# One set of weight sums fewer, a longer wait for the early sums in the output projection, and half a weight unit moved behind the turned tiles

## The chip, the core and the metric

The kernel runs on one core of one Trainium2 chip. The metric is the device time of one execution in microseconds; lower is better. Before the change the median of three runs is 1202.67 us (1201.94 to 1203.7). The profile shown below is of one further execution, which took 1203.26 us; its span, from the first to the last instruction that the profile shows, is 1201.4 us. So 1.86 us lie around the span.

Engine names: PE is the matmul engine (PEld its weight loads), DVE the vector engine, ACT the scalar engine, POOL is used mostly for its DMA queue, and SP only issues DMAs.

## What is computed

One decoder layer over 256 tokens of width 2048, all in float32. The part that matters here, cut from the reference:

```python
h += concat(A, B) @ W_o               # A: latent attention, B: block attention
h += SwiGLU(RMSNorm(h))               # W_gate, W_up: 2048 x 5632, W_down: 5632 x 2048
h += sigmoid(RMSNorm(h) @ W_pg) * (p[i] @ W_pe)
final RMSNorm
```

## The kernel before

Every weight is read once from memory, in **units** of 256 weight rows by 1024 columns (1 MB), and multiplied with the 256 tokens, which stay on the chip. A float32 product is made of three matmuls of reduced precision (`three`, lines 400 to 402): the high part of the activation times the high part of the weight, low times high, high times low. So each weight tile must first be split into two parts: ACT writes the high part (`split_hi`, line 352, a cast), DVE the low part (`split_lo`, line 363, a subtraction). The parts go into a ring of slots (`ringh`/`ringl`, then `moreh`/`morel`, then the two halves of `most`), and a slot is free again when PE has read it. The third matmul of a product (line 402) is the one that reads the low part.

Stages follow each other in program order: the attention's projections and attention itself, the output projection in two column halves `wo0` and `wo1` (eight units each), the norm and transposes for the feed-forward part, then gate and up groups in column blocks of 1024: `g0`, `u0`, `g1`, one half of down (`d10`), `u1`, the other half (`d11`), `g2` and so on.

Some units of a gate or up group are multiplied by **Strassen's scheme**: seven products of half size instead of eight (`seven`). Such a unit, written S, needs sums of its weight quarters, and is split in four jobs: "11 22" (two quarters, 1024 columns), "21" (512), and the sums "t1 t3" and "t4 t2" (1024 each). PE takes them in four turns: two products (6 matmuls), one (3), two (6), two (6), so 21 matmuls for a unit. The sums are made in one of two ways:
- **in line**: DVE makes them in place, in the raw tile, between its splits of the same unit: line 362 (1024 columns), then lines 365 and 366 (512 each);
- **early**: the generator `early_sums` (lines 370 to 388) loads the weights over POOL's queue during attention and output projection (line 378), waits until PE has been given a set number of columns (`wait()`), lets DVE make the sums (lines 384 to 386, `wsums`) and stores them to memory (line 388). Later the unit is loaded as three quarters (lines 224 and 225) and its sums (line 226), into two raw tiles. `EARLY` (line 1044) says how many S units of each group are early: 14 before.

`S["two"]` chooses the wait of `early_sums`: 57344 columns in the groups ga, q0 and u0 (the latent's up-projection of the attention part also has the names u0 and u1), else 34816. PE starts a matmul of 512 columns every 0.227 us in the trace.

Each engine's list of instructions is written out by hand, in program order: the last loop of the program walks over the units; for each it collects the jobs that may be split now (`todo`, at most two or three units ahead), issues their splits, then the unit's products, and then the loads of raw tiles that have come free. Of the last unit of the first up group `u0`, the splits are woven between its products (`WOVEN`). That unit ends the group: its evacuation adds the Strassen part (line 430, `U`), multiplies with the gate (line 1012, `stage`), and PE turns the result (`ff_transpose`, line 1032) into banks, from which ACT and DVE write the **turned tiles** `ffTh` (line 121) and `ffTl` (line 122). The next group `g1` has the units "6 S0 S1 S2 S3 S4 S5 7", of which S4 and S5 are early. The matmuls of unit S0 write banks that `ffTl` must have read first.

In the output projection, the products of `wo0` are added to `h` by DVE (line 899, four instructions, one for each bank), and the first products of `wo1` write the same four banks again. Behind it come the statistics of the first norm (lines 169 to 180), ACT's scaling (line 952) and PE's transposes (line 138).

Of the kernel before, what the change touches and what calls it, by code (L numbers as in the profile page):

```python
# [35 lines left out]
def kernel(ctx, tc, x, p, positions, attn_norm, w_in, kv_norm, w_ukv, w_o, ffn_norm,  # L36
# [31 lines left out]
    def load_x(dst, c0, c1):  # L68
        nc.sync.dma_start(dst[:, :, c0:c1], x_v[:, :, c0:c1])
# [114 lines left out]
    units = []  # L184
# [28 lines left out]
    def load(i):  # L213
        if i >= len(units) or units[i].again or i in raw:
            return
        u = units[i]
        u.asked = asking[0]
        while max(u.raw, u.raw2) >= len(raws):
            n = len(raws)
            raws.append(big.tile([128, 2048], F32, name=f"raw{n}", tag=f"f1{'hl'[n - 3]}"))  # L220
        if u.early:
            r = raws[u.raw][:, 0:1536]
            (w, c0, _), k0 = u.srcs[0], u.ks[0] * 128
            nc.sync.dma_start(r[:, 0:512], w[k0:k0 + 128, c0:c0 + 512])
            nc.sync.dma_start(r[:, 512:1536], w[k0 + 128:k0 + 256, c0:c0 + 1024])
            nc.sync.dma_start(raws[u.raw2], u.early)
            raw[i] = r.rearrange("q (a c) -> q a c", a=3)
            return
        n = sum(c1 - c0 for _, c0, c1 in u.srcs)
        nk = len(u.ks)  # L230
        r = raws[u.raw][:, 0:nk * n].rearrange("q (k c) -> q k c", k=nk)
        o = 0
        for w, c0, c1 in u.srcs:
            k0 = u.ks[0]
            nc.sync.dma_start(r[:, :, o:o + c1 - c0],
                              w[k0 * 128:(k0 + nk) * 128, c0:c1].rearrange("(k q) c -> q k c", q=128))
            o += c1 - c0
        raw[i] = r
# [6 lines left out]
    jobs, turns = [], []  # L245
# [124 lines left out]
    def early_sums(tag, enough, wait):  # L370

        made = 0
        while todo_early and made < enough:
            u = todo_early.pop(0)
            made += 1
            f = big.tile([128, 4, 512], F32, name="wsums", tag=tag)
            (w, c0, _), k0 = u.srcs[0], u.ks[0] * 128
            nc.gpsimd.dma_start(f.rearrange("q (k a) c -> q k (a c)", k=2),
                                w[k0:k0 + 256, c0:c0 + 1024].rearrange("(k q) c -> q k c", q=128))
            since = columns[0]  # L380
            while columns[0] < since + wait() or S["crowded"]:
                yield 1
            tt = nc.vector.tensor_tensor
            tt(f[:, 0:2], f[:, 1:2].to_broadcast([128, 2, 512]), f[:, 0:4:3], op=ALU.subtract)
            tt(f[:, 3], f[:, 3], f[:, 0], op=ALU.subtract)
            tt(f[:, 2], f[:, 2], f[:, 3], op=ALU.subtract)
            u.early = dram.tile([128, 2048], F32, name=f"wsums{u.name}{u.idx}")
            nc.gpsimd.dma_start(u.early, f.rearrange("q a c -> q (a c)"))

    def split(jb):  # L390
        if not jb.cast:
            split_hi(jb)
        split_lo(jb)
# [85 lines left out]
    def sums_of(parts, k0, pairs, at, tag="vb"):  # L479

        for n, kk in enumerate(pairs):
            both = big.tile([128, 2, 2, SEQ], F32, name="both", tag=tag)
            whole, some = both[:, 0], both[:, 1]
            h, l = (x[:, kk - k0:kk - k0 + 2] for x in parts)
            tt = nc.vector.tensor_tensor
            tt(whole, h.bitcast(F32), l.bitcast(F32), op=ALU.add)
            a11, a21, a12, a22 = (whole[:, i, t * 128:(t + 1) * 128] for i in range(2) for t in range(2))
            hi, lo = (aT[i][:, at + 2 * n:at + 2 * n + 2] for i in range(2))
            four = some.rearrange("q a (b c) -> q (a b) c", b=2)
            tt(four[:, 0], a21, a22, op=ALU.add)  # L490
            tt(four[:, 1], four[:, 0], a11, op=ALU.subtract)
            tt(four[:, 2], a21, a11, op=ALU.subtract)
            tt(four[:, 3], a12, four[:, 1], op=ALU.subtract)
            split_psum(hi, lo, some)
            yield 1
# [10 lines left out]
    def add(gen, wait=0, front=False):  # L506
        tasks.insert(0 if front else len(tasks), [wait, gen])
# [143 lines left out]
    S = {"done": 0, "doneB": 0}  # L651
# [389 lines left out]

    wg, wup, wd = w_gate[0], w_up[0], w_down[0]

    EARLY = dict(u0=2, g1=2, u1=2, g2=1, u2=2, g3=1, u3=2, u4=2)

    def mixed(name, order=((0, 0), (1, 0), (0, 1), (1, 1))):

# [5 lines left out]
                    adding=tuple(i for i, x in enumerate(pairs) if x[-1] == "+"),  # L1053
                    early=sevens[-EARLY.get(name, 0):] if name in EARLY else (), order=list(order) if sevens else None,
                    swap=not sevens, deep=True)
# [34 lines left out]
    def h_back():  # L1090
        S["h"] = big.tile([128, NT, D], F32, name="h", tag="xh")
        nc.gpsimd.dma_start(S["h"], S["hd"])
# [150 lines left out]
    for n in range(3):  # L1243
        for i in range(4):
            if n:
                u = Unit()
# [42 lines left out]
    nxt, j = 2, 0  # L1289
    coming = 3  # L1290

    def loads(end):

        nonlocal coming
        while coming < end and (units[coming].again or units[coming].behind < (
                jobs[nxt].unit if nxt < len(jobs) else len(units))):
            load(coming)
            coming += 1

    for i, u in enumerate(units):  # L1300
        asking[0] = i
        if i < wide:
            load(i + 3)
        S["two"] = u.name in ("ga", "q0", "u0")
        S["crowded"] = u.name == "v" and u.idx > 0 or u.name == "wo0" and u.idx < 4
        if u.name == "ga" and u.idx == 5:
            todo_early.extend(x for x in units if x.early)
            add(early_sums("f0l", 2, lambda: 53248))
        if u.name == "ga" and u.idx == 8:
            add(early_sums("more_sums", 99, lambda: 57344 if S["two"] else 34816))  # L1310
        if u.name == "g1" and u.idx == 0:
            S["mid"] = S.pop("turned")
        if u.name == "wo0":
            S["twice"] = u.idx < 4
        if i < 5:
            load_x(xt, 768 + 256 * i, 1024 + 256 * i)
        if u.name == "dl0" and u.idx == 1:
            h_back()
        if u.name == "dl0" and u.idx == 0:
            add(sums_of(ffT[4], 32, LAST_SUMS, 8), 5)  # L1320
        if u.name == "dl0" and u.idx == 2:
            add(p_load())
        if u.name == "pg0" and u.idx == 0:
            fg_load()
        if u.name == "wo0" and u.idx < 4:
            step()
        for n in range(max(1, len(u.turns))):
            todo, late = [], []
            while i not in raw and u.turns:
                loads(i + 1)  # L1330
            while nxt < len(jobs) and jobs[nxt].unit in raw and jobs[nxt].wait < j and jobs[nxt].unit <= i + (3 if i > 1 else 1) and \
                    (jobs[nxt].unit <= i + 2 or i >= wide and units[jobs[nxt].unit].asked < i) and \
                    not (u.sevens_end and 0 <= n < 3 and jobs[nxt].unit > i + 1) and \
                    not (jobs[nxt].unit > i + 2 and i + 1 < len(units) and units[i + 1].name == "u0" and units[i + 1].mixed and units[i + 1].last):
                todo.append(jobs[nxt])
                nxt += 1
            weave = u.name in WOVEN and u.last
            if "mid" in S and not u.strassen and u.mixed or u.sevens_end and n == 3 or weave:
                late = [jb for jb in todo if jb.turn > j]
                todo = [jb for jb in todo if jb.turn <= j]  # L1340
            if i >= 5:
                high_parts(todo + late if weave else todo)
            if i == 2:
                product(u, [0])
            if n % 2 == 0:
                step()
            for jb in todo:
                if i < 3:
                    for c0, c1 in units[jb.unit].chunks:
                        split_hi(jb, c0, c1, len(jb.kks))  # L1350
                        split_lo(jb, c0, c1, len(jb.kks))
                    continue
                split(jb)
            while posts:
                posts.pop()()
            if u.strassen:
                seven(u, n)
            elif i == 2:
                product(u, [1])
            else:  # L1360
                product(u, [kk for jb in u.turns[n] for kk in jb.kks] if u.turns else range(len(u.ks)), late if weave else ())
            if "mid" in S and not u.strassen and u.mixed and 2 * u.idx + n >= 0 and len([*S["mid"]]) >= 0:
                S.pop("mid")
            high_parts(late)
            for jb in late:
                split(jb)
            loads(len(units) if i >= wide else wide + 3)
            j += not u.again
# [25 lines left out]
```

## Time and profile before

| | |
|---|---|
| median of three runs | 1202.67 us |
| the profiled execution | 1203.26 us |
| its span | 1201.4 us |
| DVE busy | 948.4 us (79%) |
| ACT busy | 712.6 us (59%) |
| POOL busy | 57.3 us (5%) |
| read from memory, written | 254.08 MB, 27.26 MB |

Busy time is the time in which an engine works on some instruction. The views used below are: the page (busy shares, and the clock that was granted to PE in 40 slices of the span), the list of waits by engine, the timeline (start in us, length in us, engine, line, operation, output and inputs, count of merged instructions; in brackets the engine's idle time before and what ended it), the same work grouped by shape in a window, the chain of work that ended last, and busy times by window. A row that merges several instructions gives the time from the start of the first to the end of the last.

### The profile page before, as it was taken

Reading aid. Unit: us, or ns where it says so; the run is one execution under the profiler, and the core shown is the slowest. Engines: PE = TensorE matmul, PEld = TensorE weight load, DVE = VectorE, ACT = ScalarE, POOL = GpSimd, SP = SyncE. Lnnn points to the kernel's source line nnn. Section 1 sums busy time; section 2 is a strip of 40 time slices with the busy share of each in tenths; the row PEclk is TensorE's granted clock in tenths of the full one; section 3 lists DMA queues with packets and bytes.
Section 4 is the critical chain, followed back from the end, with each engine's and each line's share of the span. In section 5 each row is a group of like instructions: output and inputs, shape, how many; then the busy total and the mean of one; then the engine's idle time right before and its main releaser. Section 6 shows DMA issues by size and latency. Waiting matters only on the chain.

```text
span 1201.4 us, 14608 instructions
## 1 busy us (share of the span) xinstructions
PE 1177.2 (98%) x5480; PEld 983.9 (82%) x5480; DVE 948.4 (79%) x1119; ACT 712.6 (59%) x908; POOL 57.3 (5%) x80
## 2 busy tenths in 40 slices
PE   9999999999979999899999999999999999999996
PEld 7888888899868888688888888888888888888886
DVE  5675756776556687998999899989998999897474
ACT  6735745456546656475757675756566665565453
POOL 5310000000000000000000000000000000000000
PEclk9999999999989999899999999999999999999998
DMA  8896877755675677296887788787959795936631
GB/s 300 283 339 215 283 284 255 273 184 212 226 299 194 252 231 291 102 333 197 320 235 261 221 314 238 258 248 272 264 201 266 253 290 189 358 126 228 209 105 71
DMA packets 87799, 290.69 MB, mean 242 GB/s; under 512 B 5740, under 2 KB 10144, under 8 KB 82864
## 3 DMA queue, kind: packets, MB, share of 16 engines
q1 hardware_dynamic: 77984, 240.94, 56.4%
q0 software_dynamic: 9456, 48.29, 14.7%
q8 instruction: 43, 0.70, 0.2%
q10 hardware_dynamic: 288, 0.52, 0.1%
q14 instruction: 28, 0.23, 0.1%
HBM read 254.08 MB, written 27.26 MB: 234 GB/s over the span
## 4 chain that ended last, share of the span: by engine, by line
PE 94%; DVE 3%; DMA 2%; ACT 0%; issue 0%; SPq 0%; DVEq 0%
PE bank L400 30%; PE bank L402 30%; PE bank L401 30%; PE bank L138 1%; DMA wsumsu<-wsums 1%; PE bank L593 1%; DMA wsums<-in_w_up 1%; PE bank L1032 1%; DVE ringl L363 1%; PE bank L714 1%; DMA x<-in_x 1%; PE bank L622 1%; PE bank L616 0%; PE bank L596 0%; PE bank L623 0%
## 5 line engine op out<-in xcount | busy, mean ns | idle before, releaser
L352 ACT CAST ringh<-raw 128x1024 fp32r<-128x1024 f32 (+4 forms) x307 | 372.7, 1249 | 279.2 <-PE bank L401 117.4
L363 DVE TENSOR_TENSOR ringl<-raw,ringh 128x1024 fp32r<-128x1024 f32 (+4 forms) x307 | 443.9, 1468 | 110.9 <-ACT ringh L352 108.7
L400 PE MATMUL bank<-ringh,aT 128*128 128x512 f32 (+3 forms) x713 | 275.0, 386 | 0.0
L402 PE MATMUL bank<-ringl,aT 128*128 128x512 f32 (+3 forms) x713 | 270.5, 379 | 0.2 <-DVE ringl L363 0.2
L401 PE MATMUL bank<-ringh,aT 128*128 128x512 f32 (+3 forms) x713 | 270.0, 379 | 0.0
L402 PEld LDWEIGHTS bank<-ringl,aT 128*128 128x128 f32 x713 | 133.9, 188 | 25.5 <-DVE ringl L363 1.1
L400 PEld LDWEIGHTS bank<-ringh,aT 128*128 128x128 f32 x713 | 134.2, 188 | 23.6 <-ACT aT L124 0.3
L401 PEld LDWEIGHTS bank<-ringh,aT 128*128 128x128 f32 x713 | 134.1, 188 | 23.4
L352 ACT CAST moreh<-raw 128x1024 fp32r<-128x1024 f32 (+2 forms) x70 | 79.8, 1174 | 22.5 <-DVE raw L362 9.2
L363 DVE TENSOR_TENSOR morel<-raw,moreh 128x1024 fp32r<-128x1024 f32 (+2 forms) x66 | 85.5, 1317 | 0.6
L352 ACT CAST most<-raw 128x1024 fp32r<-128x1024 f32 (+2 forms) x58 | 56.7, 1006 | 42.1 <-DVE raw L362 16.0
L400 PE MATMUL bank<-ringh,ffTh 128*128 128x512 f32 x204 | 79.4, 389 | 0.0
L401 PE MATMUL bank<-ringh,ffTl 128*128 128x512 f32 x204 | 79.4, 389 | 0.0
L402 PE MATMUL bank<-ringl,ffTh 128*128 128x512 f32 x204 | 79.4, 389 | 0.0
L363 DVE TENSOR_TENSOR most<-raw,most 128x1024 fp32r<-128x1024 f32 (+2 forms) x58 | 66.3, 1164 | 2.4 <-ACT most L352 2.3
L362 DVE TENSOR_TENSOR raw<-raw 128x1024 f32<-128x1024 f32 x50 | 61.2, 1225 | 1.7
L402 PEld LDWEIGHTS bank<-ringl,ffTh 128*128 128x128 f32 x204 | 38.3, 188 | 7.9
L401 PEld LDWEIGHTS bank<-ringh,ffTl 128*128 128x128 f32 x204 | 38.3, 188 | 7.9
L400 PEld LDWEIGHTS bank<-ringh,ffTh 128*128 128x128 f32 x204 | 38.3, 188 | 7.9
L400 PE MATMUL bank<-most,aT 128*128 128x512 f32 x88 | 35.2, 400 | 5.9 <-DVE ffTl L122 5.9
L366 DVE TENSOR_TENSOR raw<-raw 128x512 f32<-128x512 f32 x50 | 34.6, 692 | 1.7
L402 PE MATMUL bank<-most,aT 128*128 128x512 f32 x88 | 34.7, 395 | 0.0
(353 smaller groups left out, 1970.7 us busy)
## 6 DMA issues: line engine op xcount, KB each, us to landing
raw<-in_w_down SPq DMA_DIRECT2D x44, 1024.0 KB, 7.4
raw<-in_w_gate SPq DMA_DIRECT2D x36, 1024.0 KB, 7.7
raw<-in_w_up SPq DMA_DIRECT2D x30, 1024.0 KB, 8.7
raw<-in_w_in SPq DMA_DIRECT2D x40, 512.0 KB, 4.7
raw<-in_w_o SPq DMA_DIRECT2D x16, 1024.0 KB, 5.4
raw<-in_w_ple_gate SPq DMA_DIRECT2D x16, 1024.0 KB, 5.0
wsums<-in_w_up POOLq DMA_DIRECT2D x10, 1024.0 KB, 6.1
wsumsu<-wsums POOLq DMA_DIRECT2D x10, 1024.0 KB, 4.8
```

Of the source, the lines that this page charges most:

```text
L138: nc.tensor.transpose(b[:, (2 * i + t) * 128:(2 * i + t + 1) * 128], part[:, t, i * 128:(i + 1) * 128], ident)
L352: nc.scalar.copy(h[:, :, c0:c1], r[:, :, c0:c1])
L362: tt(f[:, 0:2], f[:, 1:2].to_broadcast([128, 2, 512]), f[:, 0:4:3], op=ALU.subtract)
L363: tt(l[:, :, c0:c1], r[:, :, c0:c1], h[:, :, c0:c1].bitcast(F32), op=ALU.subtract)
L366: tt(f[:, 2], f[:, 2], f[:, 3], op=ALU.subtract)
L400: nc.tensor.matmul(b, xh, h, start=start, stop=False)
L401: nc.tensor.matmul(b, xl, h, start=False, stop=False)
L402: nc.tensor.matmul(b, xh, l, start=False, stop=stop)
L593: nc.tensor.matmul(s[:, c0:c0 + nk], qT[:, q * 128:(q + 1) * 128], kT[:, 0:nk], start=True, stop=qpe is None)
L622: nc.tensor.matmul(o[:, 0:256], v(0), pT[:, 0:256], start=True, stop=False)
L714: nc.tensor.transpose(b[:, (2 * i + t) * 128:(2 * i + t + 1) * 128], src[:, t, col(i0 + i):col(i0 + i) + 128], ident)
L1032: nc.tensor.transpose(b[:, (2 * i + t) * 128:(2 * i + t + 1) * 128], st[:, t, (k + i) * 128:(k + i + 1) * 128], ident)
```

## The change

Three edits. `EARLY` takes one S unit of `u0` instead of two (S3; S2 now makes its sums in line), so there are 13 early sets. The long wait of 57344 columns now holds in `wo0` and `wo1` too, where it was 34816. And the rule for which jobs wait beyond `u0`'s end is a function: as before, at the last unit but one of `u0` no job further than two units ahead is taken; new is that at its last unit none of S1 of `g1` is taken, and of S0 only the first two jobs.

```diff
-    EARLY = dict(u0=2, g1=2, u1=2, g2=1, u2=2, g3=1, u3=2, u4=2)
+    EARLY = dict(u0=1, g1=2, u1=2, g2=1, u2=2, g3=1, u3=2, u4=2)
...
+    end_u0 = next(i for i, u in enumerate(units) if u.name == "g1") - 1
+
+    def may_wait(i, jb):
+        return i == end_u0 - 1 and jb.unit > i + 2 or i == end_u0 and (
+            jb.unit > i + 2 or jb.unit == i + 2 and jb.kind in ("t1 t3", "t4 t2"))
...
-        S["two"] = u.name in ("ga", "q0", "u0")
+        S["long"] = u.name in ("ga", "q0", "u0", "wo0", "wo1")
...
-            add(early_sums("more_sums", 99, lambda: 57344 if S["two"] else 34816))
+            add(early_sums("more_sums", 99, lambda: 57344 if S["long"] else 34816))
...
-                    not (jobs[nxt].unit > i + 2 and i + 1 < len(units) and units[i + 1].name == "u0" and units[i + 1].mixed and units[i + 1].last):
+                    not may_wait(i, jobs[nxt]):
```

PE's order of instructions is the same before and after. What moves on DVE, first at the end of `wo0` (raw_112 to raw_114 are the three raw tiles of that stage, bank_77 to bank_80 the banks of `wo0`):

```order
 L363 TENSOR_TENSOR ringl<-raw_113,ringh 128x2048
-L384 TENSOR_TENSOR wsums<-wsums 128x1024
-L385 TENSOR_TENSOR wsums<-wsums 128x512
-L386 TENSOR_TENSOR wsums<-wsums 128x512
 L363 TENSOR_TENSOR morel<-raw_114,moreh 128x2048
 L899 TENSOR_TENSOR h<-h,bank_77 128x512
```

```order
 L899 TENSOR_TENSOR h<-h,bank_80 128x512
 L363 TENSOR_TENSOR ringl<-raw_112,ringh 128x2048
+L384 TENSOR_TENSOR wsums<-wsums 128x1024
+L385 TENSOR_TENSOR wsums<-wsums 128x512
+L386 TENSOR_TENSOR wsums<-wsums 128x512
 L169 TENSOR_REDUCE rs_v<-ssh 128x2
```

One set of sums has gone from ahead of the four additions to `h` to behind them and behind one more split, ahead of the norm's statistics. The set that stood behind the statistics before is gone, as the last of 14.

Second, on DVE at the end of `u0`, before the change (raw_2926 holds S0 of `g1`, raw_112 holds S1):

```order
L366 TENSOR_TENSOR raw_2926<-raw_2926 128x512
L363 TENSOR_TENSOR ringl<-raw_2926,ringh 128x1024 x2
L363 TENSOR_TENSOR ringl<-raw_112,ringh 128x1024
L362 TENSOR_TENSOR raw_112<-raw_112 128x1024
L363 TENSOR_TENSOR ringl<-raw_112,ringh 128x512
L365 TENSOR_TENSOR raw_112<-raw_112 128x512
L366 TENSOR_TENSOR raw_112<-raw_112 128x512
L122 TENSOR_TENSOR ffTl<-bank_77,ffTh 128x512
```

And after it (here raw_2917 holds S0, raw_2919 S1):

```order
L366 TENSOR_TENSOR raw_2917<-raw_2917 128x512
L122 TENSOR_TENSOR ffTl<-bank_77,ffTh 128x512
L122 TENSOR_TENSOR ffTl<-bank_78,ffTh 128x512
L122 TENSOR_TENSOR ffTl<-bank_79,ffTh 128x512
L122 TENSOR_TENSOR ffTl<-bank_80,ffTh 128x512
L363 TENSOR_TENSOR ringl<-raw_2917,ringh 128x1024 x2
L363 TENSOR_TENSOR ringl<-raw_2919,ringh 128x1024
L362 TENSOR_TENSOR raw_2919<-raw_2919 128x1024
```

The seven splits and sums that stood between S0's last sum and the first turned tile now stand behind the four turned tiles. On ACT the four casts to `ffTh` move in the same way, ahead of the casts of S0's last two jobs and of S1.

Third, on DVE within `u0`, S2 with its in-line sums, after the change (raw_114 holds S2); before, the two splits shown stood there without the three sums between and behind them, and S2's other two jobs split a second raw tile:

```order
L363 TENSOR_TENSOR ringl<-raw_114,ringh 128x1024
L362 TENSOR_TENSOR raw_114<-raw_114 128x1024
L363 TENSOR_TENSOR ringl<-raw_114,ringh 128x512
L365 TENSOR_TENSOR raw_114<-raw_114 128x512
L366 TENSOR_TENSOR raw_114<-raw_114 128x512
```

So DVE gets three instructions more for S2, and the same three fewer in the output projection.

## The prediction

> **What bounds the kernel now.** First the page, then the waits of PE.
>
> ```profile
> span 1201.4 us, 14608 instructions
> PE 1177.2 (98%) x5480; PEld 983.9 (82%) x5480; DVE 948.4 (79%) x1119; ACT 712.6 (59%) x908; POOL 57.3 (5%) x80
> PEclk9999999999989999899999999999999999999998
> PE bank L400 <- DVE h L899: 6.4, 1, 6.4
> PE bank L400 <- DVE ffTl L122: 5.9, 1, 5.9
> ```
>
> PE is busy 98% of the span, so only what holds PE up can change the time. Inside the kernel it waits for DVE twice: once for the additions to `h` (the output projection's two halves meet), once for the turned tiles (`u0` meets `g1`). The slices with a lower clock, the twelfth and the seventeenth of 30 us each, are those two places. So a wait costs more than its length; PE's timeline gives the whole price:
>
> ```profile
> 337.10 0.39 PE L402 MATMUL bank<-ringl,oBh 128*128 128x512 f32 x1
> 339.82 0.39 PE L402 MATMUL bank<-ringl,oBh 128*128 128x512 f32 x1
> 346.63 0.77 PE L400 MATMUL bank<-ringh,oMh 128*128 128x512 f32 x1 [6.42 <-DVE h L899]
> ...
> 351.03 0.63 PE L401 MATMUL bank<-ringh,oMl 128*128 128x512 f32 x1
> 351.46 0.45 PE L402 MATMUL bank<-ringl,oMh 128*128 128x512 f32 x1
> 351.75 0.40 PE L400 MATMUL bank<-ringh,oMh 128*128 128x512 f32 x1
> ```
>
> From 337.10 to 339.82 are 12 steps of 0.227 us. After the wait they are 0.43 (351.03 to 351.46): half speed, for eleven matmuls. The 13th matmul behind the wait starts at 351.75; without wait it would at 339.82 + 13 x 0.227 = 342.77. **Price of the first wait: 8.98 us**, 6.6 of it idle and 2.4 slow matmuls.
>
> ```profile
> 487.91 0.39 PE L402 MATMUL bank<-morel,aT 128*128 128x512 f32 x1
> 494.21 0.79 PE L400 MATMUL bank<-most,aT 128*128 128x512 f32 x1 [5.91 <-DVE ffTl L122]
> 501.05 0.39 PE L400 MATMUL bank<-ringh,aT 128*128 128x512 f32 x1
> 513.06 0.39 PE L402 MATMUL bank<-ringl,sumsmore_sums 128*128 128x512 f32 x1
> ```
>
> S0 of `g1` is 21 matmuls from 494.21; S1 begins as the 22nd, at 501.05, instead of 487.91 + 22 x 0.227 = 492.90. **Price of the second: 8.15 us.**
>
> **The output projection.** What DVE and ACT did there:
>
> ```profile
> 332.61 1.91 ACT L352 CAST moreh<-raw 128x2048 fp32r<-128x2048 f32 x1 [1.52 <-DMA raw<-in_w_o]
> 331.10 9.78 DMA wsums<-in_w_up
> 331.13 2.29 DVE L363 TENSOR_TENSOR ringl<-raw,ringh 128x2048 fp32r<-128x2048 f32 x1 [3.15 <-ACT ringh L352]
> 341.00 1.23 DVE L384 TENSOR_TENSOR wsums<-wsums 128x1024 f32<-128x1024 f32 x1 [7.58 <-DMA wsums<-in_w_up]
> 343.60 2.29 DVE L363 TENSOR_TENSOR morel<-raw,moreh 128x2048 fp32r<-128x2048 f32 x1
> 345.80 2.48 DVE L899 TENSOR_TENSOR h<-h,bank 128x512 f32<-128x512 f32 x4
> 350.92 2.29 DVE L363 TENSOR_TENSOR ringl<-raw,ringh 128x2048 fp32r<-128x2048 f32 x1 [2.64 <-ACT ringh L352]
> ```
>
> DVE stood 7.58 us at the head of a sum whose weights landed at 340.9, with the split and the four additions queued behind it. In the new order the split comes at once: its cast ends at 334.5, so it runs to 336.8. The last unit of `wo0` is 24 matmuls that end at 340.05, six for each bank, so the first bank is done 18 x 0.227 = 4.1 us earlier, at 336.0. Its addition (0.62 us, a quarter of 2.48) ends at 337.4, 2.6 us before PE wants the bank; the last one ends near 340.7, while PE is still 18 matmuls from its bank. Saved: the whole 8.98.
>
> What is late next? The moved sum: four additions to 340.7; 2.64 us, as before (350.92), for ACT's squares and cast; the split to 345.7; then the sum, whose data have been there for 4.8 us. It ends at 345.7 + 2.6 (341.00 to 343.60) = 348.3. Behind it on DVE wait the norm's statistics, then ACT's scaling, then PE's transposes:
>
> ```profile
> 353.13 0.15 DVE L169 TENSOR_REDUCE rs_v<-ssh 128x2 f32<-128x4 f32 x1
> 356.30 0.90 ACT L952 ACTIVATE stage<-h,rs 128x256 f32<-128x256 f32 x2
> 365.56 0.44 PE bank L138 x4
> ```
>
> From the statistics' start to the scaling 3.2 us, scaling 0.9: ready at 352.4. PE reaches the transposes at 365.56 - 8.98 = 356.6. The moved sum is covered by 4.2 us. The 14th set, its load and store on POOL's queue and its 2.6 us of DVE vanish; DVE has 7.6 us of idle there in that one row, so they are worth nothing on the path. SP's loads of `in_w_o` wait for raw tiles that DVE frees, and come earlier by what DVE gains.
>
> **S2 in line.** It adds lines 362, 365 and 366 to DVE in `u0`, as S1 has them:
>
> ```profile
> 445.53 1.23 DVE L362 TENSOR_TENSOR raw<-raw 128x1024 f32<-128x1024 f32 x1
> 447.27 0.69 DVE L365 TENSOR_TENSOR raw<-raw 128x512 f32<-128x512 f32 x1
> 447.99 0.69 DVE L366 TENSOR_TENSOR raw<-raw 128x512 f32<-128x512 f32 x1
> 455.52 2.60 DVE L363 TENSOR_TENSOR ringl<-raw,ringh 128x1024 fp32r<-128x1024 f32 x2 [0.21 <-ACT ringh L352]
> 463.03 0.39 PE L402 MATMUL bank<-ringl,sumsatt 128*128 128x512 f32 x1
> 469.64 0.69 DVE L468 TENSOR_TENSOR U<-U,bank 128x512 f32<-128x512 f32 x1 [3.42 <-ACT moreh L352]
> ```
>
> 1.23 + 0.69 + 0.69 = 2.6 us. S2's third job, the first of two at 455.52, ended near 456.8 and was read at 463.03: 6.2 us of slack, of which 2.6 go. Before the group's sums (line 468) DVE idles 3.42 us until PE has finished, so the delay ends there. Cost nothing; 2.6 if that idle time were gone. On SP two loads (three quarters, 0.75 MB, and sums, 1 MB) become one of 1 MB.
>
> **The turned tiles.** The chain here is DVE's:
>
> ```profile
> 477.00:510.00 33.00, 27.09 (x120) 22.14 (x119) 32.50 (x39) 12.85 (x16) 0.00 (x0) 0.90 0.38 137
> L363 DVE TENSOR_TENSOR ringl<-raw,ringh 128x1024 fp32r<-128x1024 f32 x7 | 8.3, 1219 | 0.0
> 477.05 0.69 DVE L430 TENSOR_TENSOR U<-U,bank 128x512 f32<-128x512 f32 x1
> 486.80 3.56 DVE L363 TENSOR_TENSOR ringl<-raw,ringh 128x1024 fp32r<-128x1024 f32 x3
> 493.48 2.48 DVE L122 TENSOR_TENSOR ffTl<-bank,ffTh 128x512 fp32r<-128x512 f32 x4
> 509.21 5.36 DVE L363 TENSOR_TENSOR ringl<-raw,ringh 128x1024 fp32r<-128x1024 f32 x5
> 484.99 1.05 ACT L352 CAST ringh<-raw 128x1024 fp32r<-128x1024 f32 x1 [9.58 <-DVE raw L362]
> 487.88 2.04 ACT L121 CAST ffTh<-bank 128x512 fp32r<-128x512 f32 x4
> 483.66 1.91 PE L1032 MATMUL bank<-ident,stage 128*128 128x128 f32 x16
> ```
>
> (The first row is a window: length, then busy time of PE, PEld, DVE, ACT, POOL; DVE has 32.50 of 33.) In the new order the turned tiles take the place at 486.80. Their casts no longer stand behind a cast that waits for DVE: ACT idled 9.58 us there, the transposes start at 483.66, so four casts of 0.51 us are done near 486.2. The first `ffTl` ends at 486.80 + 0.69 = 487.5, before 488.14, when PE wants the bank. The wait is gone, with 0.6 us to spare.
>
> But DVE's work is only reordered, and it has no idle time from 477.05 on. S3's third job, the first of the five at 509.21, still ends at 509.21 + 1.22 = 510.43. Before, PE read it at 513.06, with **2.63 us to spare**; without the wait PE wants it at 513.06 - 8.15 = 504.91. So PE now waits 5.52 us for low parts, a piece at a time: first at S1's third job, wanted at 501.05 + 11 x 0.227 - 8.15 = 495.4 and split at 486.80 + 2.4 (tiles) + 6.68 (the rows from 486.80 to 493.48, now behind them) + 1.22 = 497.1, so 1.7 us late; the rest at those of S2 and S3. S4 and S5, with early sums, leave DVE three instructions less, and there it catches up. Saved here: 8.15 - 5.52 = **2.63 us**.
>
> Sum: 8.98 + 2.63 = 11.6 us. The profiled execution took 1203.26 (its span and 1.86 around it), which gives 1191.6; it lies 0.59 above the median of the runs shown, against which the result will be held: **1191.0 us**.
>
> The trace has no row for PE's clock during such short waits. Below: no loss; above: 2.4 us, the slow matmuls behind the first wait. I take nothing: the clock row has no third low slice before the last. The Trainium skill, "TensorE: Matmul & The Clock Gate", section "HAM oscillation — how this bites in real kernels", has the clock halve after gaps of over about 3.4 us; the two waits here agree, and by it the new ones of under 2 us cost no clock. Against that, its section "A second HAM failure mode: psum-queue depth-cycling" has frequent small idle times make the clock swing too; no run here shows that, and it would make the sum about 1193.4.
>
> **The rivals.**
> - *Short waits slow the clock.* For: half speed after both long waits. Against: each is under 2 us. Slow matmuls are hidden while DVE is late anyway; only those behind the last wait count, 2.4 us: 1193.4. Chance 0.12.
> - *DVE's lateness does not bind* (PE reads low parts later than I count, or DVE runs faster): both prices saved in full, 1202.67 - 17.1 = 1185.5. Against: the 32.50 of 33. Chance 0.05.
> - *The turned tiles gain nothing*, or S2's 2.6 us find no cover: 1202.67 - 8.98 = 1193.7, or 1191.0 + 2.6 = 1193.6. For: 0.6 us to spare is little. Chance 0.12.
> - *The moved sum's data comes late, and the wait moves to the norm.* DVE then holds the statistics, and PE stands at the transposes. Sum, statistics and scaling are 2.6 + 3.2 + 0.9 = 6.7 us, so it begins when the data land after 356.6 - 6.7 = 349.9, 18.8 us after the issue at 331.10 (it took 9.78), and the kernel is slower than before if they land after 349.9 + 11.6 = 361.5. In the old order the same load shared the DMA engines with three weight loads, now with one more. Between 1193 and 1203: chance 0.05; slower: 0.03.
>
> **How the numbers follow.** Forecast 1191.0, chance 0.63, its own range 1189.5 to 1192.5. With the two cases near 1193.5 the range 1187.5 to 1194.5 leaves out the full gain below and the late data above, 0.13, and some error of the forecast. A measurement of this kernel tells 0.2% (2.4 us) from no change; the forecast is 1.0%. Faster by over 0.2%: 0.94; within: 0.03; slower: 0.03.
>
> **What would show it.** In the profile after: no wait of PE for `h`; no long wait for `ffTl`; no slice of low clock in either place; three waits of PE (line 402) for `ringl` or `most` of 1 to 2 us each in `g1`, about 5.5 us together; DVE without idle time there; the sum (line 384) without a wait for DMA. Wrong would be: a wait at the transposes, slow matmuls in `g1`, or waits in `g1` that add up to 8 us or to nothing.

## The result, and the profile after

| | before | after |
|---|---|---|
| median of five runs each, side by side | 1202.29 us (1201.77 to 1203.7) | 1191.73 us (1190.96 to 1193.17) |
| ratio | | 0.9912, 95% interval 0.9897 to 0.9926 |
| span of the profiled execution | 1201.4 us | 1190.4 us |

The kernel is 10.6 us faster; 1191.0 was forecast. The page after (span, busy time of the engines, granted clock of PE in 40 slices), and the list of PE's waits:

```profile
span 1190.4 us, 14607 instructions
PE 1175.2 (99%) x5480; PEld 980.9 (82%) x5480; DVE 947.5 (80%) x1119; ACT 711.9 (60%) x908; POOL 56.0 (5%) x78
PEclk9999999999999999999999999999999999999999
PE bank L402 <- DVE ringl L363: 2.4, 2, 1.2
PE bank L113 <- DVE junk L108: 2.0, 1, 2.0
PE bank L402 <- DVE most L363: 1.2, 1, 1.2
```

The wait on line 113 stands within the first 10 us, before and after alike; it is left out of the lists below. The two long waits, for `h` and for `ffTl`, are gone, and with them the two slices of lower clock. Three waits of 1.2 us have come in their place, all on line 402, the matmul that reads a low part. Here they are on PE's timeline in `g1`, the first one with the starts around it:

```profile
479.07 0.39 PE L400 MATMUL bank<-most,aT 128*128 128x512 f32 x1
...
485.71 0.39 PE L402 MATMUL bank<-ringl,aT 128*128 128x512 f32 x1
486.07 0.50 PE L400 MATMUL bank<-ringh,sumsatt 128*128 128x512 f32 x1
486.40 0.40 PE L401 MATMUL bank<-ringh,sumsatt 128*128 128x512 f32 x1
487.99 0.50 PE L402 MATMUL bank<-ringl,sumsatt 128*128 128x512 f32 x1 [1.19 <-DVE ringl L363]
488.32 0.39 PE L400 MATMUL bank<-ringh,sumsatt 128*128 128x512 f32 x1
...
494.70 0.50 PE L402 MATMUL bank<-most,sumsatt 128*128 128x512 f32 x1 [1.17 <-DVE most L363]
...
501.72 0.50 PE L402 MATMUL bank<-ringl,sumsmore_sums 128*128 128x512 f32 x1 [1.18 <-DVE ringl L363]
```

The row at 479.07 is the first matmul of S0, which had waited 5.9 us for `ffTl`; it now starts in step. A short wait costs more than its 1.2 us: from 485.71 to 488.32 PE starts four matmuls in 2.61 us instead of 4 x 0.227 = 0.91, so 1.70 us are lost. The matmuls just before and behind this wait start 0.33 to 0.36 us apart as well, not 0.227; near the other two waits single steps are up to 0.56 us long. Summing what the longer steps have over 0.227, over all of PE's starts between 480 and 580 us, gives **5.8 us** lost in `g1`. This sum is used below for the experiments too.

Against before, the start at 501.72 is 513.06 - 501.72 = 11.3 us earlier, and the span 11.0 us shorter: the whole gain stands at S3's third job in `g1`, and what lies behind it changes the sum by 0.3 us. The stretch of `g1`, as a window (length, busy time of PE, PEld, DVE, ACT, POOL, then the granted clock, DMA share, GB/s):

```profile
476.00:512.00 36.00, 32.35 (x136) 24.33 (x135) 35.34 (x39) 23.25 (x28) 0.00 (x0) 1.00 0.46 155
```

DVE is busy for 35.34 of 36 us: it is the engine that sets the pace here. The clock is 1.00 in spite of three waits within 14 us.

### The profile page after: what moved, and what is told of

Read it like the earlier page. It is cut to its first block, busy times and chain, and to the rows that moved or that the text cites. A ratio compares the mean times of both kernels' runs of the same rounds, so it can differ in the third digit from the quotient of the medians.

```text
span 1190.4 us, 14607 instructions
## 1 busy us (share of the span) xinstructions
PE 1175.2 (99%) x5480; PEld 980.9 (82%) x5480; DVE 947.5 (80%) x1119; ACT 711.9 (60%) x908; POOL 56.0 (5%) x78
## 4 chain that ended last, share of the span: by engine, by line
PE 96%; DVE 3%; issue 1%; ACT 0%; DMA 0%; SPq 0%; DVEq 0%; ACTq 0%
PE bank L402 30%; PE bank L400 30%; PE bank L401 30%; PE bank L138 1%; PE bank L593 1%; DVE ringl L363 1%; PE bank L1032 1%; PE bank L622 1%; PE bank L714 1%; PE bank L616 0%; PE bank L596 0%; PE bank L623 0%; DMA x<-in_x 0%; DVE U L430 0%; DVE raw L365 0%
## 5 line engine op out<-in xcount | busy, mean ns | idle before, releaser
L366 DVE TENSOR_TENSOR raw<-raw 128x512 f32<-128x512 f32 x51 | 35.3, 692 | 1.8
L365 DVE TENSOR_TENSOR raw<-raw 128x512 f32<-128x512 f32 x51 | 34.9, 684 | 0.0
L400 PE MATMUL bank<-most,aT 128*128 128x512 f32 x88 | 34.6, 393 | 0.0
```

The source lines that it names most:

```text
L400: nc.tensor.matmul(b, xh, h, start=start, stop=False)
```

## The experiments

Each is the changed kernel with one edit, and each is held against the kernel before, run on the same chip.

### The shorter wait for the sums again

```diff
-        S["long"] = u.name in ("ga", "q0", "u0", "wo0", "wo1")
+        S["long"] = u.name in ("ga", "q0", "u0")
```

> The changed kernel with the old wait of 34816 columns in the output projection: one set of sums stands ahead of the four additions to h again; 13 sets and the new order at g1 stay. Theory (the wait of DVE for that set's weights, with the additions queued behind it, is what costs): PE waits about 6.4 us for h and then runs eleven matmuls at half speed, price 9.0 us, so about 1200.7 us. Rival (it is the 14th set that was one too many, in DVE time and memory traffic): about 1191.7 us, no wait for h.

Measured: 1201.01 us (1200.07 to 1202.41), ratio 0.9989 (0.998 to 0.9998). PE's waits:

```profile
PE bank L400 <- DVE h L899: 6.7, 1, 6.7
PE bank L402 <- DVE ringl L363: 2.4, 2, 1.2
...
PE bank L402 <- DVE most L363: 1.2, 1, 1.2
```

The wait for `h` is back and the short waits stay, with 13 sets. So the first wait goes because the sum stands elsewhere, not because there is a set less, and it is worth 1201.01 - 1191.73 = 9.3 us (the forecast priced it at 8.98; here the wait itself is 6.7 us instead of 6.4).

### The old rule for which jobs may wait

```diff
-        return i == end_u0 - 1 and jb.unit > i + 2 or i == end_u0 and (
-            jb.unit > i + 2 or jb.unit == i + 2 and jb.kind in ("t1 t3", "t4 t2"))
+        return i == end_u0 - 1 and jb.unit > i + 2
```

> The changed kernel with the old rule for the jobs at u0's end: the turned tiles stand again behind S0's last two jobs and S1's first two. Theory (DVE's work ahead of S3's third job in g1 is the same in both orders, so only the 2.6 us to spare there were won): PE waits about 5.9 us for ffTl, half speed after it, none of the three short waits in g1; 2.6 us slower than the changed kernel, about 1194.3 us. Rival (the long wait's whole price was won): 8.1 us slower, about 1199.9 us.

Measured: 1194.01 us (1193.09 to 1194.53), ratio 0.9931 (0.9918 to 0.9943). In this kernel PE has the long wait again and no short one; the window over `g1` shows the lower clock:

```profile
PE bank L400 <- DVE ffTl L122: 5.9, 1, 5.9
476.00:512.00 36.00, 30.10 (x126) 24.45 (x124) 35.66 (x40) 22.76 (x27) 0.00 (x0) 0.91 0.46 160
```

The second edit is worth 2.3 us, not the 8.15 that its wait had cost: the forecast had 2.63. The 9.3 and the 2.3 add up to 11.6, and both edits together measured 10.6. Part of that is the longer wait in the run before; the rest is within the scatter of the runs, which lie 2 us and more apart for either kernel.

### Only S1 behind the turned tiles, S0 ahead

```diff
-        return i == end_u0 - 1 and jb.unit > i + 2 or i == end_u0 and (
-            jb.unit > i + 2 or jb.unit == i + 2 and jb.kind in ("t1 t3", "t4 t2"))
+        return i >= end_u0 - 1 and i <= end_u0 and jb.unit > i + 2
```

> The changed kernel with all four jobs of S0 ahead of the turned tiles, and only S1 behind them. Theory (the last late piece in g1 sets the end, not the first): ffTl comes 2.3 us later and PE waits some 1.6 us for it; the first of the short waits in g1 shrinks by as much, the third piece is split at the same time; no change against the changed kernel, about 1191.7 us, within 0.5. Rival (waits add up): 1.6 us slower, about 1193.3 us.

Measured: 1191.92 us (1191.85 to 1192.03), ratio 0.9914 (0.99 to 0.9928), as the changed kernel.

```profile
...
PE bank L400 <- DVE ffTl L122: 1.7, 1, 1.7
PE bank L402 <- DVE most L363: 1.2, 1, 1.2
PE bank L402 <- DVE ringl L363: 1.2, 1, 1.2
```

One of the three short waits has become a wait for `ffTl` at S0. Whatever stands first, DVE has the same work ahead of S3's third job, and PE waits the same time for it, in other places.

### Fourteen sets with the long wait: a miss

```diff
-    EARLY = dict(u0=1, g1=2, u1=2, g2=1, u2=2, g3=1, u3=2, u4=2)
+    EARLY = dict(u0=2, g1=2, u1=2, g2=1, u2=2, g3=1, u3=2, u4=2)
```

> The changed kernel with S2 of u0 early again: 14 sets, the last of them now among the norm's transposes in the second half of the output projection, where DVE is idle. Theory (S2's in-line sums were hidden by idle DVE time, and so is the 14th set now): about 1191.7 us, within 0.5; DVE idle before line 468 longer by 2.6 us. Rival (a 14th set holds up the norm, so 13 are needed): 2.6 us or more slower, from 1194.3 us on, with a wait of PE at the transposes (line 138).

Measured: 1197.72 us (1196.47 to 1198.89), ratio 0.9962 (0.9948 to 0.9975): 6.0 us slower than with 13 sets. The expectation looked only at DVE in `u0`. The loss is in the output projection. Timelines of DVE, POOL, ACT and PE there, those of PE last:

```profile
376.11 1.22 DVE L384 TENSOR_TENSOR wsums<-wsums 128x1024 f32<-128x1024 f32 x1
...
379.08 0.55 POOL L388 DMA_DIRECT2D wsumsu<-wsums  x1 [24.88 <-DVE wsums L386]
...
385.24 0.62 ACT L121 CAST sumsmore_sums<-stage 128x512 fp32r<-128x512 f32 x1 [7.98 <-DMA wsumsu<-wsums]
...
385.89 0.69 DVE L122 TENSOR_TENSOR sumsmore_sums<-stage,sumsmore_sums 128x512 fp32r<-128x512 f32 x1 [5.58 <-ACT sumsmore_sums L121]
386.50 2.28 DVE L363 TENSOR_TENSOR morel<-raw,moreh 128x2048 fp32r<-128x2048 f32 x1
...
385.67 0.39 PE L401 MATMUL bank<-moreh,aT 128*128 128x512 f32 x1
388.84 0.80 PE L402 MATMUL bank<-morel,aT 128*128 128x512 f32 x1 [2.78 <-DVE morel L363]
...
392.31 0.39 PE L401 MATMUL bank<-moreh,aT 128*128 128x512 f32 x1
...
396.46 0.95 PE L138 MATMUL bank<-ident,stage 128*128 128x128 f32 x4 [0.78 <-ACT stage L952]
```

With the longer wait the 14th sum comes at 376 us, amid the norm. Its store is issued at 379.1, and its tile `wsums` has the same place in the on-chip memory (the tag `more_sums`, line 376) as the norm's last tile of sums, `sumsmore_sums` (line 944). So ACT, about to write that tile, stands 7.98 us until the store has landed; DVE's low part and its split behind it wait with it, and PE waits for the split. The wait also costs clock, as the window behind it shows (the third number from the end):

```profile
388.74:392.15 3.41, 3.31 (x8) 2.63 (x9) 3.41 (x5) 0.53 (x1) 0.00 (x0) 0.50 1.03 422
```

From 385.67 to 392.31 PE makes nine steps in 6.64 us instead of 9 x 0.227 = 2.04, so 4.6 us are lost; against the starts of the changed kernel another 1.3 go at the late transposes (396.46), and the transposes ahead of the 14th sum lose nothing. In the kernel before, the short wait had brought the 14th sum out at 357 us.

### Fourteen sets, the last one with the short wait

```diff
-            add(early_sums("more_sums", 99, lambda: 57344 if S["long"] else 34816))
+            add(early_sums("more_sums", 99, lambda: 57344 if S["long"] and todo_early else 34816))
```

This together with the edit of the run before.

> 14 early sets as in e4, but the last of them waits the short number of columns (34816) in the output projection, and only the 13 before it wait the longer one. Theory: what cost 6 us in e4 was not the 14th set itself but its late store. Its sum ran at 376.1 us, its store was issued at 379.1, and the tile lies in the place that the norm's last summed tile takes, so ScalarE's cast on line 121 waited 8.0 us for the store to land, and the splits and the additions to h behind it came late. With the short wait the last sum comes about 12 us earlier, near 364 us, and its store has landed near 372, ahead of the cast that after has at 378.6. So the time is that of after, 1191.7 (1191.0 to 1192.9), with no wait of ScalarE for that store and no PE wait near 386 to 400 us. Rival: any 14th set after the norm's start costs, because its 2.6 us of VectorE time or its 2 MB of transfers come amid the norm and the last unit of the projection: then 1194 to 1198, with PE waits between 364 and 400 us.

Measured: 1193.13 us (1192.53 to 1193.41), ratio 0.992 (0.9906 to 0.9933).

```profile
363.37 1.23 DVE L384 TENSOR_TENSOR wsums<-wsums 128x1024 f32<-128x1024 f32 x1
...
368.70 0.95 PE L138 MATMUL bank<-ident,stage 128*128 128x128 f32 x4 [0.77 <-ACT stage L952]
...
380.22 0.62 ACT L121 CAST sumsmore_sums<-stage 128x512 fp32r<-128x512 f32 x1 [1.69 <-DVE stage L158]
```

ACT's cast waits for DVE again, not for the store, and 4.6 of the 6.0 us are back. By PE's starts, all that the late store had cost near 386 to 397 us is gone, and 1.6 us are new: the sum now comes at 363 us, ahead of the transposes at 368.70, and its 2.6 us of DVE work make them late (0.77 us of wait there, and longer steps at these transposes and the next). So the theory holds for the store, and the rival for the place to which the sum moved.

### Sets moved to `g1`

If the short waits are DVE's lateness, they go with DVE's in-line sums in `g1`. Four kernels with the number of early sets in each group changed (a group not named has none), in the order of the texts below:

```diff
-    EARLY = dict(u0=1, g1=2, u1=2, g2=1, u2=2, g3=1, u3=2, u4=2)
+    EARLY = dict(u0=1, g1=3, u1=2, g2=1, u2=2, g3=1, u3=2, u4=1)
+    EARLY = dict(u0=1, g1=4, u1=2, g2=1, u2=2, g3=1, u3=1, u4=1)
+    EARLY = dict(g1=4, u1=2, g2=1, u2=2, g3=1, u3=2, u4=1)
+    EARLY = dict(g1=3, u1=2, g2=1, u2=2, g3=1, u3=2, u4=2)
```

Three in `g1`, one in `u4`:

> after, with three early sets for g1 instead of two and one for u4 instead of two: 13 as before. S3 of g1 then has its sums ahead of time, and VectorE loses 2.6 us of sums just ahead of the low part that PE waits for at 501.72 us. Theory: the three short waits in g1 are VectorE's lateness, each adds about 1.8 us (1.2 idle, and the end of the job before it and the start lie in the rest) and taking S3's sums away removes the third: 1191.7 - 1.9 = 1189.8 (1189.2 to 1190.6), two short waits in g1 left. u4's second set, in line again, costs VectorE 2.6 us where it now idles 2.5 us at 1036 us: nothing, or 1 us. Rival: VectorE stays late enough that the next job takes the wait over, or u4's in-line sums make a new wait there: 1191.2 to 1193.

Four in `g1`, one in `u3` and one in `u4`:

> after, with four early sets for g1, one for u3 and one for u4: 13 as before. S2 and S3 of g1 have their sums ahead of time. Theory: two of the three short waits go, S1's alone is left: 1191.7 - 3.7 = 1188.0 (1187.3 to 1189.2). The sums in line again in u3 and u4 meet 2.8 and 2.5 us of idle VectorE time (at 913 and 1036 us) and cost nothing to 1 us. Rival: they make new waits of PE in u3 and u4: 1190 to 1192, with the waits shown there.

Four in `g1`, none in `u0`, one in `u4`:

> after, with four early sets for g1, none for u0 and one for u4: 13 as before. Another place to take the set from: u0's last sums are in line too, and VectorE there idles 3.05 us ahead of the group's sums (line 468), of which they take 2.6. Theory: as e7, 1188.0 (1187.3 to 1189.2). Rival: u0's low part with the in-line sums is read before VectorE has it, a wait of PE near 455 to 462 us of 1 to 2.6 us: 1189 to 1190.6.

Three in `g1`, none in `u0`:

> after, with three early sets for g1 and none for u0: 13 as before, nothing taken from u3 or u4. By the gaps between PE's starts, the three short waits of g1 cost 5.8 us in after, 3.8 in e6 and 1.7 in e7, so 2.0 for each set moved to g1; the set taken from u3 or u4 gave 1.6 to 1.7 back through one new short wait each. In e8 u0's stretch shows no gap. Theory: u0 is the one place where a set can be had for nothing, since only its last two S units are in line one behind the other: 1191.7 - 2.0 = 1189.7 (1189.0 to 1190.4), two short waits in g1 and none elsewhere. Rival: what e8 gained came from another place, and u0 gives back as much as u3 and u4: 1191.4.

| | lost by PE in `g1` | new short waits elsewhere | median (range) | ratio to before |
|---|---|---|---|---|
| the changed kernel | 5.8 us | none | 1191.73 | 0.9912 (0.9897 to 0.9926) |
| three, `u4` one | 3.8 us | `u4` 1.4 us | 1191.44 (1191.0 to 1191.58) | 0.9906 (0.9893 to 0.992) |
| four, `u3` and `u4` one | 1.7 us | `u3` 1.6 us, `u4` 1.7 us | 1191.02 (1190.67 to 1191.45) | 0.9903 (0.989 to 0.9917) |
| four, `u0` none, `u4` one | 1.8 us | `u4` 1.7 us | 1188.93 (1188.31 to 1189.8) | 0.9886 (0.9873 to 0.99) |
| three, `u0` none | 3.6 us | none | 1189.53 (1188.86 to 1189.82) | 0.9892 (0.9877 to 0.9907) |

In `g1` the theory holds: 2.0 to 2.2 us go with each set. The first two kernels came out at their rivals' times, not at the 1189.8 and 1188.0 expected: the cover in `u3` and `u4` was wrong. Of the two rows of idle time that the texts named, 913 us lies within `u4`, ahead of its last three in-line units, and 1036 us some 100 us behind it. In the kernel with four in `g1` and one in each of `u3` and `u4`, PE's timeline has these two new waits:

```profile
810.61 0.50 PE L402 MATMUL bank<-ringl,sumsmore_sums 128*128 128x512 f32 x1 [1.15 <-DVE ringl L363]
...
936.22 0.50 PE L402 MATMUL bank<-ringl,sumsmore_sums 128*128 128x512 f32 x1 [1.17 <-DVE ringl L363]
```

DVE's timeline in `u3` of that kernel shows why its idle time was no cover:

```profile
784.76 1.23 DVE L363 TENSOR_TENSOR ringl<-raw,ringh 128x1024 fp32r<-128x1024 f32 x1 [4.42 <-ACT ringh L352]
786.02 1.23 DVE L362 TENSOR_TENSOR raw<-raw 128x1024 f32<-128x1024 f32 x1
...
792.77 1.22 DVE L362 TENSOR_TENSOR raw<-raw 128x1024 f32<-128x1024 f32 x1
...
799.51 1.23 DVE L362 TENSOR_TENSOR raw<-raw 128x1024 f32<-128x1024 f32 x1
...
806.27 1.22 DVE L362 TENSOR_TENSOR raw<-raw 128x1024 f32<-128x1024 f32 x1
...
810.89 1.23 DVE L363 TENSOR_TENSOR ringl<-raw,ringh 128x1024 fp32r<-128x1024 f32 x1 [0.33 <-ACT ringh L352]
```

The 4.42 us lie **ahead** of the row of units, when DVE stands for ACT's cast. Inside it the sums follow each other every 6.75 us without a gap: an in-line unit takes 6.75 us of DVE, while PE's 21 matmuls take 21 x 0.227 = 4.8. So DVE falls back 2.0 us with each such unit and lives on the lead that the ring of slots gives it; with a fourth unit in this row PE waits. The count alone doesn't decide: in the changed kernel a row of four, with sums at 857, 864, 871 and 877 us, brings no wait. How large the lead is at the head of each row wasn't measured. In `u0` no such wait comes:

```profile
459.29 0.69 DVE L468 TENSOR_TENSOR U<-U,bank 128x512 f32<-128x512 f32 x1 [0.30 <-PE bank L402]
```

That is the kernel with four in `g1` and none in `u0`; DVE's 3.05 us of idle time before this row (in the changed kernel) have shrunk to 0.30, by the 2.6 us of one set, and PE's starts from 430 to 470 us show no loss. With three in `g1` and none in `u0` the time is 2.2 us below the changed kernel, where 2.0 had been expected, and PE's list has just two short waits left:

```profile
...
PE bank L402 <- DVE ringl L363: 1.2, 1, 1.2
PE bank L402 <- DVE most L363: 1.2, 1, 1.2
```

**The two kernels without an early set in `u0` are the fastest found: 1188.93 us with four in `g1` and one in `u4`, 1189.53 us with three in `g1`; that is 2.8 and 2.2 us below the changed kernel, and 13 below the one before.** Their ranges overlap, and the table's losses give them nearly the same gain (5.8 - 1.8 - 1.7 = 2.3 and 5.8 - 3.6 = 2.2 us), so which of them is faster stays open. That the first one fell within the range expected for it is in part luck: the text left out the wait in `u4`.

### Both together

The first of these two with a 14th set for `u4`, which waits the short number of columns.

> e8 with u4's second set early again, so 14 sets, the last of them with the short wait as in e5. Arithmetic: e8's 1188.9, less 1.7 for the short wait of u4 that goes, plus 1.1 to 1.4 for the 14th set's sum amid the norm's transposes: 1188.3 to 1188.6, which these rounds can hardly tell from e8; the waits can: S1's short wait in g1, none in u4, one of 0.8 us at the norm's transposes. Rival: the 14th set's store is late here too and ScalarE waits for it: 1192 to 1193.

Measured: 1189.55 us (1188.24 to 1190.4), ratio 0.9891 (0.9874 to 0.9907), about 1 us above what was expected. PE's starts show no loss in `u4`, and the wait at the norm's transposes is there (0.72 us); what the one gives, the other takes. In the profiled execution the norm's second transposes, ahead of the 14th sum, already come 0.7 us later than in the changed kernel (362.95 against 362.29 us). That delay arises near 138.8 us, where PE waits 0.43 us for ACT (line 863); why it does so in this execution is not known, so whether this kernel and the two before it differ at all stays open.

## Why the prediction was right

- **First wait.** The additions to `h` were to end near 340.7, with 2.6 us to spare for the first bank; the last started at 340.22 and ended at 340.91. PE's last matmul of `wo0` and the first of `wo1` (it reads `oMh`), 0.23 us apart:

```profile
339.79 0.39 PE L402 MATMUL bank<-ringl,oBh 128*128 128x512 f32 x1
340.02 0.39 PE L400 MATMUL bank<-ringh,oMh 128*128 128x512 f32 x1
```

  The price, 8.98 us forecast, was 9.3 by the first experiment.
- **The moved sum.** Start 345.7, end 348.3, scaled rows ready at 352.4, PE at the transposes at 356.6 were forecast. After, on DVE, ACT and PE:

```profile
340.22 0.69 DVE L899 TENSOR_TENSOR h<-h,bank 128x512 f32<-128x512 f32 x1 [0.67 <-PE bank L402]
343.56 2.29 DVE L363 TENSOR_TENSOR ringl<-raw,ringh 128x2048 fp32r<-128x2048 f32 x1 [2.65 <-ACT ringh L352]
345.77 1.22 DVE L384 TENSOR_TENSOR wsums<-wsums 128x1024 f32<-128x1024 f32 x1
348.36 0.15 DVE L169 TENSOR_REDUCE rs_v<-ssh 128x2 f32<-128x4 f32 x1
350.65 0.90 ACT L952 ACTIVATE stage<-h,rs 128x256 f32<-128x256 f32 x2
356.35 0.60 PE L138 MATMUL bank<-ident,stage 128*128 128x128 f32 x4
```

  The sum has no wait for its data, and PE finds the rows 4.8 us old; they came 0.9 us earlier than forecast, since from the statistics to the scaling it took 2.3 us, not 3.2. The rival of late data fell.
- **The 14th set.** "Worth nothing on the path" was argued for its old place, behind the statistics at 357 us. The text missed that the longer wait would have carried that set on into the norm, so that leaving it out is a condition of the first edit: with it, 6.0 us are lost. The forecast's number doesn't hang on it, since the change leaves the set out; the reason that the text gave for leaving it out wasn't the one that counts.
- **S2 in line.** Costed at nothing, right; even a second set more in `u0` costs nothing. The reason given, the idle time before line 468, was only half of it: in `u3` and `u4` idle time was no cover. What these runs point to is the lead that DVE still has at the end of a row of in-line units, before its next rest.
- **The turned tiles.** The first `ffTl` was to end 0.6 us before PE wants its bank, at 488.14 - 8.98 = 479.16. The four started at 477.73, so the first ended near 478.4 by its share of 0.69 us, and PE's matmul started at 479.07, without a wait:

```profile
475.23 2.06 ACT L121 CAST ffTh<-bank 128x512 fp32r<-128x512 f32 x4 [12.28 <-PE bank L1032]
477.73 2.47 DVE L122 TENSOR_TENSOR ffTl<-bank,ffTh 128x512 fp32r<-128x512 f32 x4
```

- **What is given back.** 5.52 us were forecast, beginning with 1.7 at S1's third job; 5.8 were lost, 1.70 at the first wait. The places and the cause were right, as the runs with sets moved to `g1` show: each in-line set less takes one wait away. One thing in the text was read too simply: the three waits listed add up to 3.6 us, not 5.5. The rest is in longer steps around them, which the list doesn't hold.
- **The clock.** Taken as no loss, against a rival of 2.4 us: the window shows 1.00. "DVE's lateness does not bind" (1185.5) fell with the three waits.
- **The size.** Forecast 11.6 us off, measured 10.6 in the medians and 11.0 in the spans. Term by term, the same matmuls of PE start at 339.82 before and 339.79 after ahead of the first wait, at 351.75 and 342.74 behind it, at 501.05 and 483.89 where S1 of `g1` begins, and at 513.06 and 501.72 at S3's third job. So the gain is 9.01 us, then 17.16, then 11.34: the prices were 9.01 and 8.15 us (8.98 and 8.15 forecast), and 5.82 were given back (5.52 forecast).

## What to carry to other kernels

Where two engines run nearly level, a wait taken from the one is worth only what the other was ahead when it next delivers: measure that lead at the last point of the stretch (here 2.63 us before S3's third job) before counting the price of the wait. In these runs idle time of the slower engine covered added work where it lay behind that work and before the next reader, and not where it lay ahead of the stretch. And when a piece of work is put off, look at what shares its buffer: a late store can hold an engine that never reads the data.

## What the hardware showed unexpectedly

Short waits didn't slow the clock: three, each with 1.57 to 1.59 us from start to start, within 14 us, at a granted clock of 1.00; nor did the wait of 1.7 us for `ffTl` in the run with S0 ahead. One of 5.9 us brought the window's mean down to 0.91. The Trainium skill, "TensorE: Matmul & The Clock Gate", section "HAM oscillation — how this bites in real kernels", puts the limit at idle gaps above about 3.4 us. The waits of 5.9 us and more, and those of 1.7 us and less, agree; the one of 2.78 us in the run with fourteen sets doesn't, for behind it the clock was 0.50 for 3.41 us. So if the length of a wait alone decides, which no run here settles, the limit lay between 1.7 and 2.78 us in these runs. The swing by frequent small idle times, which the Trainium skill has on the same page in section "A second HAM failure mode: psum-queue depth-cycling", doesn't show here. What the three short waits of `g1` do cost, beside themselves, is 0.5 to 0.9 us each in the steps around them (three to six steps of 0.27 to 0.56 us instead of 0.227). Why these steps are longer at full clock stays open; no run was made on it.
